# More groups of seven products in the down projection of one hybrid layer

## The chip, the cores and the metric

One core of one Trainium2 chip runs the whole layer as one program. The metric is the device time of one execution in microseconds, lower is better; the kernel before took 1129.32 us (median of 3 runs, 1128.81 to 1129.38).

## The reference, cut to what matters

```python
h2 = rmsnorm(x, norm_ffn)                                  # x: 256 tokens x 2048
x = x + jnp.square(jax.nn.relu(h2 @ w_up)) @ w_down        # w_up 2048 x 8192, w_down 8192 x 2048
return rmsnorm(x, final_norm)
```

Ahead of it stand the projection `w_in`, a chunkwise mLSTM, a forgetting attention, a convolution branch and `w_out`; the change leaves them alone. All is float32.

## The kernel before, in words

**One product.** TensorE multiplies float32r, a float32 rounded to fewer bits. To keep float32 accuracy each operand is split in two: `hi` is the rounded value (written by ScalarE, ACT below) and `lo` what is left (a subtraction on VectorE, DVE below). A product of activations x and weights w is then three matmuls: x_hi by w_hi, x_hi by w_lo, x_lo by w_hi (`mul`, L57). Weights come from HBM in pieces of 128 x 1024 floats (tile `raw`, eight buffers, loaded at L349 by SP's queue), and each piece is split into one `hi` and one `lo`, of which there are five buffers each (NHL = 5): a piece can be split at most five steps ahead of TensorE.

**The feed-forward part.** The 8192 hidden columns are worked in four quarters q of 2048. In each quarter the up projection makes four blocks of 512 hidden columns, and then the down projection multiplies them with 2048 rows of `w_down`. Its 2048 output columns go in two pairs p of 1024 columns; a pair is two blocks of 512 columns, b0 (called x in the order below) and b1 (called y). A pair runs over the four chunks c of 512 hidden values. PSUM has eight banks, four with the tag `mm` and four with `mx`; a block of the down projection holds two (one for each half of the 256 tokens), a block of the up projection four. The two tags change places from one block of the up projection to the next, and from quarter to quarter for the down projection.

**Plain units and groups of seven.** A chunk of a pair is either two plain units (x and y: two steps each, 24 matmuls of 128x512 each) or one group s of seven products after Strassen's scheme (`seven_matmuls`: seven steps of six matmuls, 42 in all). The group needs sums and differences of weight pieces (`sum_task`, L396, four subtractions of 128x1024 on DVE) and of activations (`x_sums`), and seven `hi` and seven `lo` where two plain units need four of each. Three of the seven products (p2, p3, p4) go straight into banks of the pair's own blocks; the four others (p1, p5, p6, p7, called SHARED) collect in four banks of the other tag over all groups of the pair. They are emptied once at the pair's end by `add_up`, one ACT copy per bank (L1361 in the first quarter; L1366, with a DVE addition for each two banks at L1370, in the later ones), and only then can the tag's next block have the banks. The table GROUPS says which chunks are groups; `pair_units` writes the order of units of a pair. In the first three quarters the first pair runs x0 y0 s1 x3 y3 s2, the second y0 x0 s1 x2 y2 x3 y3; in the last quarter the first pair runs x0 y0 s2 x1 y1 x3 y3 and the second has no group.

**What leaves the banks.** `gather` reads a finished block out of PSUM with ACT (L1412, one instruction per bank) and adds it to the residual on DVE (L1418). In the last quarter DVE reads the banks itself (L1485).

**Who sets the order.** A planner inside the kernel keeps a clock for each engine, with costs written in the code, and whenever TensorE's next step is placed it issues for ACT, DVE and POOL those tasks which are ready by its clocks, by priority. The order of TensorE's steps is fixed by `pair_units`. Every engine then runs its instructions strictly in the order issued. `room` tells the planner when PSUM banks and buffers that a step takes are free again. It has no influence on the hardware's waits, which are semaphores.

## Time and profile before

| | |
|---|---|
| median of 3 runs | 1129.32 us |
| the profiled execution, own time | 1129.26 us |
| its span, first to last instruction | 1127.2 us |
[...]
| share of the span: TensorE matmuls, weight loads | 99%, 85% |
| share of the span: DVE, ACT, POOL | 75%, 57%, 2% |
| read from HBM | 211.87 MB, 190 GB/s over the span |

The profiled execution took 0.06 us less than the median of the runs, and 2.06 us of its time lie around the span. TensorE's share counts modelled ends of pipelined matmuls, so it says that matmuls follow each other without a pause, not that each is as fast as it could be. The four down projections lie at 516 to 599, 688 to 771, 860 to 943 and 1032 to 1118 us.

### The profile page before, as it was taken

The page shows a single profiled execution, that of the slowest core. Times are in us where ns is not written, and L with a number is a line of the kernel's source. Part 1 is how long each engine was busy: PE and PEld are TensorE (multiplying, and loading weights), DVE is VectorE, ACT ScalarE, POOL GpSimd, SP SyncE. Part 2 cuts the span into 40 slices and gives each one's busy share as a digit, 9 for nine tenths or more (in the row PEclk, how much of TensorE's full clock was granted, in tenths as well). Part 3 has the DMA queues.
Part 4 walks back from the last instruction along what each step waited for, and adds up shares of the span by engine and source line. Part 5 has one row for each costly group of instructions (what it writes and reads, how often), then busy time and mean ns, then how long its engine had stood idle before and what let it go on. Part 6 is the DMA issues. An engine that isn't in the chain of part 4 may idle for free.

```text
span 1127.2 us, 15562 instructions
## 1 busy us (share of the span) xinstructions
PE 1113.7 (99%) x5836; PEld 954.9 (85%) x5836; DVE 841.0 (75%) x1125; ACT 640.3 (57%) x911; POOL 17.1 (2%) x40
## 2 busy tenths in 40 slices
PE   8999999999999999999999999999999999999996
PEld 7888788888888888888888888888888888888885
DVE  6679998887677785677975677995577997567973
ACT  6444365777775565545664554764454665454552
POOL 1000000010000000000000000000000000000000
PEclk9999999999999999999999999999999999999998
DMA  9766654657555375554776554776554677654742
GB/s 309 253 199 193 187 160 140 181 156 230 182 172 170 126 261 168 168 190 160 233 239 195 179 168 150 232 252 188 187 168 150 219 243 248 187 185 149 245 129 75
DMA packets 130820, 214.98 MB, mean 191 GB/s; under 512 B 6797, under 2 KB 48057, under 8 KB 130361
## 3 DMA queue, kind: packets, MB, share of 16 engines
q1 hardware_dynamic: 130136, 212.93, 58.8%
q8 instruction: 46, 0.75, 0.3%
q10 hardware_dynamic: 608, 1.06, 0.3%
q14 instruction: 30, 0.24, 0.1%
HBM read 211.87 MB, written 2.10 MB: 190 GB/s over the span
## 4 chain that ended last, share of the span: by engine, by line
PE 97%; DMA 1%; issue 1%; DVE 1%; ACT 0%; POOLq 0%; POOL 0%; ACTq 0%; DVEq 0%
PE mm L57 65%; PE mx L57 30%; DMA x<-in_x_dram 1%; DMA rowp<-in_norm_mix_dram 0%; PE mx L984 0%; PE mx L1323 0%; ACT hi L440 0%; PE mx L651 0%; ACT x2t L1525 0%; PE mx L1017 0%; DVE x L637 0%; DVE h L637 0%; DVE x L630 0%; ACT junk L1512 0%; POOLq L1647 0%
## 5 line engine op out<-in xcount | busy, mean ns | idle before, releaser
L461 DVE TENSOR_TENSOR lo<-raw,hi 128x1024 fp32r<-128x1024 f32 x348 | 417.8, 1222 | 218.9 <-issue 136.6
L440 ACT ACTIVATE hi<-raw 128x1024 fp32r<-128x1024 f32 x348 | 364.7, 1058 | 298.4 <-PE mm L57 183.0
L57 PE MATMUL mm<-hi,hid 128*128 128x512 f32 x520 | 163.4, 389 | 0.0
L57 PE MATMUL mm<-x,hi 128*128 128x512 f32 x640 | 156.4, 394 | 0.0
L57 PEld LDWEIGHTS mm<-x,hi 128*128 128x128 f32 x640 | 116.9, 188 | 23.1 <-ACT tmp L559 0.4
L408 ACT ACTIVATE hi<-raw 128x1024 fp32r<-128x1024 f32 x77 | 81.7, 1062 | 73.4 <-PE mm L57 31.4
L57 PE MATMUL mm<-h,hi 128*128 128x512 f32 x512 | 122.7, 391 | 0.2
L57 PE MATMUL mx<-h,hi 128*128 128x512 f32 x512 | 122.1, 390 | 0.0
L57 PEld LDWEIGHTS mm<-hi,hid 128*128 128x128 f32 x520 | 97.6, 188 | 20.2
L57 PEld LDWEIGHTS mm<-h,hi 128*128 128x128 f32 x512 | 94.1, 188 | 19.2 <-DVE x2t L1310 0.9
L57 PEld LDWEIGHTS mx<-h,hi 128*128 128x128 f32 x512 | 94.2, 188 | 18.3
L57 PE MATMUL mx<-hi,hid 128*128 128x512 f32 x328 | 104.3, 389 | 0.0
L412 DVE TENSOR_TENSOR lo<-raw,hi 128x1024 fp32r<-128x1024 f32 x77 | 93.1, 1221 | 14.0 <-ACT hi L408 13.3
L57 PE MATMUL mm<-lo,hid 128*128 128x512 f32 x260 | 101.2, 389 | 0.0
L57 PEld LDWEIGHTS mm<-x,lo 128*128 128x128 f32 x640 | 82.0, 191 | 3.2
L57 PE MATMUL mm<-x,lo 128*128 128x256 f32 x640 | 83.0, 282 | 0.0
L57 PE MATMUL mm<-hi,y 128*128 128x512 f32 x232 | 73.5, 392 | 0.0
L57 PEld LDWEIGHTS mx<-hi,hid 128*128 128x128 f32 x328 | 61.6, 188 | 12.7
L57 PEld LDWEIGHTS mx<-h,lo 128*128 128x128 f32 x512 | 65.6, 191 | 2.5
L57 PEld LDWEIGHTS mm<-h,lo 128*128 128x128 f32 x512 | 65.6, 191 | 2.5
L57 PE MATMUL mm<-h,lo 128*128 128x256 f32 x512 | 66.4, 283 | 0.0
L57 PE MATMUL mx<-h,lo 128*128 128x256 f32 x512 | 66.4, 283 | 0.0
(239 smaller groups left out, 1242.4 us busy)
## 6 DMA issues: line engine op xcount, KB each, us to landing
raw<-in_w_up_dram SPq DMA_DIRECT2D x128, 512.0 KB, 4.2
raw<-in_w_down_dram SPq DMA_DIRECT2D x128, 512.0 KB, 4.9
raw<-in_w_in_dram SPq DMA_DIRECT2D x92, 512.0 KB, 3.6
raw<-in_w_out_dram SPq DMA_DIRECT2D x32, 512.0 KB, 4.2
raw<-in_w_in_dram SPq DMA_DIRECT2D x8, 516.0 KB, 3.6
raw<-in_w_in_dram SPq DMA_DIRECT2D x4, 544.0 KB
x<-in_x_dram SPq DMA_DIRECT2D x8, 256.0 KB, 4.2
x2t<-in_x_dram SPq DMA_DIRECT2D x2, 1024.0 KB
```

The costliest lines, as they stand in the source:

```text
L57: pe.matmul(o, l, r, start=start, stop=stop, skip_group_check=True)
L408: act.activation(hl[i][0], piece(u, h), AF.Copy)
L412: dve.tensor_sub(hl[i][1], piece(u, h), hl[i][0].bitcast(F32))
L440: act.activation(hl[i][0], raws[u, h][0], AF.Copy)
L461: dve.tensor_sub(hl[i][1], raws[u, h][0], hl[i][0].bitcast(F32))
```

## The change

In the first three quarters the second pair gets a second group: its order becomes y0 x0 s1 x3 s2 y3. In the last quarter the first pair gets a second group: x0 y0 x1 s2 y1 s3. The sums of activations for chunk 3 have a buffer of their own (`fourth`, tag `zz`), and those of chunk 2 in the first three quarters are now stored packed, as chunk 1's were. In the last quarter the first two blocks are read from PSUM by `gather`. A bank's last product may now come in any group (`ends`). `room` counts all buffers that a step takes from one rotation, where it looked before at the first one for each.

```diff
--- before.py
+++ after.py
@@ -107,11 +107,13 @@
 
     def room(takes):
 
-        r = 0.0
+        r, more = 0.0, {}
         for b in takes:
             h = b.rot.hist
-            if len(h) >= b.rot.n:
-                for u in h[len(h) - b.rot.n].readers:
+            m = len(h) + more.get(id(h), 0)
+            more[id(h)] = more.get(id(h), 0) + 1
+            if m >= b.rot.n:
+                for u in h[m - b.rot.n].readers:
                     if u.fin is None:
                         return None
                     r = max(r, u.fin + LAT)
@@ -488,7 +490,10 @@
                 xl = stat[:, k, S + j * P:S + (j + 1) * P]
             else:
                 m = {"p5": 0, "p6": 1, "p3": 2, "p7": 3}[p]
-                xh, xl = (g["sums"]()[:, v_, m, ii, :] for v_ in range(2))
+                if m == 3 and g["fourth"]:
+                    xh, xl = (g["fourth"].t[:, v_, ii, :] for v_ in range(2))
+                else:
+                    xh, xl = (g["sums"]()[:, v_, m, ii, :] for v_ in range(2))
             mul(ps, xh, hi[:, ii, :], start and ii == 0, False)
             mul(ps, xh, lo[:, ii, :], False, False)
             mul(ps, xl, hi[:, ii, :], False, stop and ii == 1)
@@ -1182,7 +1187,7 @@
 
         order = [w + str(c) for c in r for w in "xy"]
         for n, c in enumerate(sv):
-            order.insert(3 * n + 2, "s%d" % c)
+            order.insert(2 * n + 3 if 3 in sv else 2 * n + 2 if swap else 3 * n + 2, "s%d" % c)
         if swap:
             order[0:2] = order[1::-1]
         for n, w in enumerate(order):
@@ -1191,7 +1196,8 @@
             rest = "".join(order[n + 1:])
             if w[0] == "s":
                 g = dict(first=c == sv[0], last=c == sv[-1], c=c,
-                         ends=(() if "x" in rest else ("p2", "p4")) + (() if "y" in rest else ("p3",)), **g_of(c))
+                         ends=(() if "x" in rest or "s" in rest else ("p2", "p4")) +
+                              (() if "y" in rest or "s" in rest else ("p3",)), **g_of(c))
                 unit(b1, src, c0 + 512, k, (), seven=(0, g))
                 unit(b0, src, c0, k, (), seven=(1, g))
             else:
@@ -1209,7 +1215,7 @@
     xsum, acc = {}, {}
     oy = seven_of(ob[2], ob[3], "mx", ys, "y")
     pair_units(ob[2], ob[3], w_out, 1024, 0, (YS,), False,
-               lambda c: dict(o=oy, sums=lambda: xsum["y"], packed=False))
+               lambda c: dict(o=oy, sums=lambda: xsum["y"], packed=False, fourth=None))
     U_FFN = len(units)
 
     x2 = {}
@@ -1237,10 +1243,12 @@
 
     z_rot, zz_rot = Rot(2), Rot(2)
 
-    def x_sums(key, c, pk, wb, d, d_lo, prev):
-
+    def x_sums(key, c, pk, wb, d, d_lo, prev, fourth=None):
+
+
+        pr = -0.95 if fourth else -1.85
         zb = Buf(z_rot)
-        m = 3 if pk else 4
+        m = 3 if pk or fourth else 4
 
         def f1():
             zb.t = sbt(pl("late"), [P, 4, S], "z", bufs=2).rearrange("p m (i t) -> p m i t", i=2)
@@ -1252,21 +1260,33 @@
             dve.tensor_sub(t[:, 3], b11, b21)
 
         def f2():
-            t = xsum[key] = sbt(pl("late"), [P, 2, m, 2, P], "xsums%d" % c, F32R)
+            n = 4 if c == 2 else m
+            t = xsum[key] = sbt(pl("late"), [P, 2, n, 2, P], "xsums%d" % (1 if fourth else c), F32R)[:, :, 0:m]
             act.activation(t[:, 0], zb.t[:, 0:m], AF.Copy)
 
         def f3():
             dve.tensor_sub(xsum[key][:, 1], zb.t[:, 0:m], xsum[key][:, 0].bitcast(F32))
 
-        d = t_dve(4 * cd(256), f1, [d] + prev, prio=-1.85, takes=[zb], uses=[wb])
-        a = t_act(ca(256 * m), f2, [d] + prev, prio=-1.85, uses=[zb])
-        r = [t_dve(cd(256 * m), f3, [a], prio=-1.85, uses=[zb])]
+        d = t_dve(4 * cd(256), f1, [d] + prev, prio=pr, takes=[zb], uses=[wb])
+        a = t_act(ca(256 * m), f2, [d] + prev, prio=pr, uses=[zb])
+        r = [t_dve(cd(256 * m), f3, [a], prio=pr, uses=[zb])]
+        if fourth:
+            def at(o):
+                return fourth.t[:, o // S]
+
+            def f4():
+                fourth.t = sbt(pl("late"), [P, 2, 2, P], "zz", F32R, bufs=2)
+                act.activation(at(0), zb.t[:, 3], AF.Copy)
+
+            a = t_act(ca(256), f4, [a], prio=pr, uses=[zb], takes=[fourth])
+            r.append(t_dve(cd(256), lambda: dve.tensor_sub(at(S), zb.t[:, 3], at(0).bitcast(F32)), [a], prio=pr,
+                           uses=[zb]))
         if pk:
             def at(o):
                 return big["hid"][:, 4 * c:4 * c + 2, o + P:o + S]
 
-            a = t_act(ca(256), lambda: act.activation(at(0), zb.t[:, 3], AF.Copy), [a, d_lo], prio=-1.85, uses=[zb])
-            r.append(t_dve(cd(256), lambda: dve.tensor_sub(at(S), zb.t[:, 3], at(0).bitcast(F32)), [a], prio=-1.85,
+            a = t_act(ca(256), lambda: act.activation(at(0), zb.t[:, 3], AF.Copy), [a, d_lo], prio=pr, uses=[zb])
+            r.append(t_dve(cd(256), lambda: dve.tensor_sub(at(S), zb.t[:, 3], at(0).bitcast(F32)), [a], prio=pr,
                            uses=[zb]))
         return r
 
@@ -1339,7 +1359,7 @@
 
 
 
-    GROUPS = {(q, p): ((1, 2), (1,))[p] if q < 3 else ((2,), ())[p] for q in range(4) for p in range(2)}
+    GROUPS = {(q, p): ((1, 2), (1, 2))[p] if q < 3 else ((2, 3), ())[p] for q in range(4) for p in range(2)}
     def packed(q, c):
         return all(c in GROUPS[q, p] for p in range(2))
 
@@ -1415,14 +1435,15 @@
         for j in range(2):
             a.append(t_act(0.62, lambda j=j: f1(j), [b.done[j], rs_t] + a[-1:], prio=-2, takes=[zb] if j == 0 else [],
                            uses=[b.bufs[j]], lag=0.3))
-        t_dve(1.22, lambda: dve.tensor_add(x2[0][:, :, cut(c)], x2[0][:, :, cut(c)], zb.t), a[1:], prio=-0.7,
-              uses=[zb])
+        return t_dve(1.22, lambda: dve.tensor_add(x2[0][:, :, cut(c)], x2[0][:, :, cut(c)], zb.t), a[1:],
+                     prio=-0.7, uses=[zb])
 
     def x2_ap(j, sl):
         return lambda: x2[0][:, j, sl]
 
     fin_t, fsq = [[], []], [[], []]
     ss3, t3 = small(8), small(2)
+    own = Buf(zz_rot)
     for q in range(4):
         t0, t1 = (("mm", "mx"), ("mx", "mm"))[q % 2]
         for c in range(4):
@@ -1452,7 +1473,8 @@
             for i in range(4):
                 chunk["hid%d" % q, 4 * c + i] = d
             if c in GROUPS[q, 0]:
-                chunk["sumshid%d" % q, c] = x_sums(c, c, packed(q, c), wb, done_zz, d, prev)
+                chunk["sumshid%d" % q, c] = x_sums(c, c, packed(q, c), wb, done_zz, d, prev,
+                                                     own if c == 3 else None)
         hid_readers = []
         def down(c, tg):
             return blk("A", 512, lambda: big["hid"], "hid%d" % q, tg)
@@ -1467,7 +1489,7 @@
             b0, b1 = bs[2 * p], bs[2 * p + 1] = down(2 * p, t0), down(2 * p + 1, t0)
             o = seven_of(b0, b1, t1, lambda: big["hid"], "hid%d" % q)
             pair_units(b0, b1, w_down, 1024 * p, KC * q, sv, p == 1,
-                       lambda c: dict(o=o, sums=lambda: xsum[c], packed=packed(q, c)))
+                       lambda c: dict(o=o, sums=lambda: xsum[c], packed=packed(q, c), fourth=own if c == 3 else None))
             got = add_up(p, q, o, q == (3, 2)[p])
             for i, t in enumerate(got):
                 shared[2 * p + i // 2, i % 2] = t
@@ -1479,10 +1501,11 @@
             if q < 3:
                 gather(b, c)
                 continue
+            moved = gather(b, c) if c < 2 else None
             for j in range(2):
                 if c == 3:
                     continue
-                d = t_dve(cd(512), lambda j=j, b=b, c=c: dve.scalar_tensor_tensor(
+                d = moved or t_dve(cd(512), lambda j=j, b=b, c=c: dve.scalar_tensor_tensor(
                     x2[0][:, j, cut(c)], b.bufs[j].t, rs2[:, j:j + 1], x2[0][:, j, cut(c)],
                     op0=OP.mult, op1=OP.add), [b.done[j], rs_t], prio=-2, uses=[b.bufs[j]])
                 if c < 3:
```

The order of ACT's instructions is where the change is seen best. The first piece is ACT's queue in the kernel before, first quarter, at the end of its second pair: `hi` are splits of weights, and the four `fnb` rows empty the four banks of the shared products (p1, p5, p6, p7) for the up projection's next block.

```order
L440 ACTIVATE hi_5532<-raw_5407 128x1024
L440 ACTIVATE hi_5545<-raw_5413 128x1024
L440 ACTIVATE hi_5557<-raw_5433 128x1024
L1361 ACTIVATE fnb_5575<-mx_5486 128x512
L440 ACTIVATE hi_5577<-raw_5495 128x1024
L1361 ACTIVATE fnb_5575<-mx_5508 128x512
L440 ACTIVATE hi_5600<-raw_5506 128x1024
L1361 ACTIVATE fnb_5575<-mx_5536 128x512
L440 ACTIVATE hi_5621<-raw_5530 128x1024
L1361 ACTIVATE fnb_5575<-mx_5521 128x512
L440 ACTIVATE hi_5640<-raw_5543 128x1024
```

The four copies stand one by one between splits of weights for the plain units x2, y2, x3 and y3, which TensorE still has to run after the group.

The same place in the change: `mx_5514`, `mx_5540` and `mx_5527` are the banks of p5, p6 and p7, `mm_5442` is a bank of the pair's first block, `mm_5395` and `mm_5396` are those of its second block, whose last unit is y3. The `hi` rows are already weights of the next up projection; `hi_5729` takes the buffer that the last step of y3 frees, being the fifth split after that step's own.

```order
L1432 ACTIVATE z_5641<-mm_5442,st_99 128x512
L442 ACTIVATE hi_5700<-raw_5620 128x1024
L442 ACTIVATE hi_5718<-raw_5630 128x1024
L1381 ACTIVATE fnb_5638<-mx_5514 128x512
L442 ACTIVATE hi_5729<-raw_5649 128x1024
L1432 ACTIVATE z_5734<-mm_5395,st_99 128x512
L1381 ACTIVATE fnb_5638<-mx_5540 128x512
L1432 ACTIVATE z_5734<-mm_5396,st_99 128x512
L1381 ACTIVATE fnb_5638<-mx_5527 128x512
L442 ACTIVATE hi_5780<-raw_5673 128x1024
L442 ACTIVATE hi_5792<-raw_5679 128x1024
```

The copies of p6 and p7 now stand behind `hi_5729` and between the two reads of block y.

The last quarter in the change, ACT's queue at the end of its first pair, which two plain blocks follow: `hi_9787` is the split for the group's last product (p4), `mx_9470` its bank, the four next `hi` belong to plain units of the next block, and `mm_9613`, `mm_9635`, `mm_9662` are shared banks; the next block takes the banks of `mm_9613` and `mm_9635` for its two halves.

```order
L410 ACTIVATE hi_9787<-raw_9633 128x1024
L442 ACTIVATE hi_9789<-raw_9656 128x1024
L442 ACTIVATE hi_9799<-raw_9671 128x1024
L442 ACTIVATE hi_9805<-raw_9683 128x1024
L442 ACTIVATE hi_9811<-raw_9701 128x1024
L1432 ACTIVATE z_9769<-mx_9470,st_99 128x512
L442 ACTIVATE hi_9818<-raw_9754 128x1024
L1386 ACTIVATE zz_9763<-mm_9635 128x512
L1386 ACTIVATE zz_9846<-mm_9662 128x512
```

The copy that frees the second bank stands behind six splits and a read, where before the change four plain units lay between the group and that block.

## Rows read from the trace of the kernel before

**Rows 1.** The page: busy time, share of the span and instructions of each engine.

```profile
PE 1113.7 (99%) x5836; PEld 954.9 (85%) x5836; DVE 841.0 (75%) x1125; ACT 640.3 (57%) x911; POOL 17.1 (2%) x40
```

**Rows 2.** Chain that ended last, first down projection: start us, us, engine, tile, line, count.

```profile
535.47 13.60 PE mm L57 x60
549.07 1.36 PE mx L57 x6
...
576.27 23.12 PE mm L57 x102
599.39 0.68 PE mx L57 x3
```

**Rows 3.** Waits of the weight loads: us in total, times, longest us.

```profile
PEld mm L57 <- DVE x2t L1310: 0.9, 2, 0.5
...
PEld mm L57 <- DVE lo L461: 0.2, 1, 0.2
```

**Rows 4.** Windows, first, second and last down projection: busy us (count) by engine, clock, DMA.

```profile
516.40:599.40 83.00, 83.00 (x367) 68.71 (x367) 69.56 (x63) 51.47 (x60) 0.00 (x0) 1.00 0.62 204
...
688.40:771.40 83.00, 83.00 (x368) 68.71 (x367) 73.96 (x67) 51.62 (x60) 0.00 (x0) 1.00 0.62 203
...
1032.40:1118.20 85.80, 85.78 (x379) 70.68 (x377) 63.73 (x74) 42.79 (x58) 0.93 (x1) 1.00 0.42 136
```

**Rows 5.** Groups by line and form: the work that groups of seven add, whole span.

```profile
L408 ACT ACTIVATE hi<-raw 128x1024 fp32r<-128x1024 f32 x77 | 81.7, 1062 | 73.4 <-PE mm L57 31.4 <-DVE raw L396 23.6 <-PE mx L57 14.6
L412 DVE TENSOR_TENSOR lo<-raw,hi 128x1024 fp32r<-128x1024 f32 x77 | 93.1, 1221 | 14.0 <-ACT hi L408 13.3
L396 DVE TENSOR_TENSOR raw<-raw 128x1024 f32<-128x1024 f32 x44 | 53.7, 1221 | 0.5
```

**Rows 6.** Timeline, DVE: start us, us, line, operation; p4's `lo` is the second.

```profile
534.77 4.62 DVE L461 TENSOR_TENSOR lo<-raw,hi 128x1024 fp32r<-128x1024 f32 x4
...
553.44 1.22 DVE L412 TENSOR_TENSOR lo<-raw,hi 128x1024 fp32r<-128x1024 f32 x1
```

**Rows 7.** Timeline, ACT: splits, reads of a block, copies of shared banks.

```profile
533.50 3.89 ACT L440 ACTIVATE hi<-raw 128x1024 fp32r<-128x1024 f32 x4
...
550.12 1.25 ACT L1412 ACTIVATE z<-mm,st 128x512 f32<-128x512 f32 x2
...
577.27 0.58 ACT L1361 ACTIVATE fnb<-mx 128x512 f32<-128x512 f32 x1
577.75 1.05 ACT L440 ACTIVATE hi<-raw 128x1024 fp32r<-128x1024 f32 x1
...
584.07 0.58 ACT L1361 ACTIVATE fnb<-mx 128x512 f32<-128x512 f32 x1
```

**Rows 8.** Timeline at p4's end and y0's start: TensorE's steps and ACT's read.

```profile
555.93 0.39 PE L57 MATMUL mm<-lo,hid 128*128 128x512 f32 x1
...
556.84 0.61 PE L57 MATMUL mm<-hi,hid 128*128 128x512 f32 x2
557.26 0.69 ACT L1412 ACTIVATE z<-mm,st 128x512 f32<-128x512 f32 x1 [0.30 <-PE mm L57]
```

**Rows 9.** Timeline, first block of the first up projection: it waits for banks.

```profile
425.32 0.41 PEld L57 LDWEIGHTS mm<-h,hi 128*128 128x128 f32 x2
425.52 1.27 DVE L1310 TENSOR_TENSOR x2t<-x2t,mm 128x512 f32<-128x512 f32 x2
425.54 4.55 PE L57 MATMUL mm<-h,hi 128*128 128x512 f32 x16
...
426.85 2.82 PEld L57 LDWEIGHTS mm<-h,hi 128*128 128x128 f32 x13 [0.41 <-DVE x2t L1310]
```

**Rows 10.** Line L349, the weight loads: who waited for them, us and times.

```profile
  ACT hi L440: 0.5, 1
  ACT hi L408: 0.2, 1
```

**Rows 11.** TensorE's timeline: its longest pause at full clock, its last matmul.

```profile
14.11 0.44 PE L651 MATMUL mx<-ident,x 128*128 128x128 f32 x2 [1.58 <-DVE x L630]
...
1117.80 0.39 PE L57 MATMUL mm<-hi,hid 128*128 128x512 f32 x1
```

**Rows 12.** Windows around both: the column behind POOL is the granted clock.

```profile
10.00:15.00 5.00, 3.42 (x29) 3.09 (x27) 4.35 (x12) 4.17 (x9) 1.50 (x5) 1.00 1.05 400
1118.50:1120.50 2.00, 0.00 (x0) 0.00 (x0) 1.27 (x4) 1.02 (x4) 0.33 (x1) 1.00 0.80 272
1121.00:1127.00 6.00, 0.00 (x0) 0.00 (x0) 0.88 (x2) 1.44 (x2) 0.11 (x1) 0.50 0.50 175
```

## Prediction

> **What bounds the kernel now.** I read the page's busy shares first [rows 1]: TensorE's matmuls fill 99% of the span, DVE 75%, ACT 57%. Then the chain that ended last, in order of time, through a down projection [rows 2]. The reader should see that it is TensorE alone, without a pause: 60 matmuls of 512 columns in 13.60 us, 6 in 1.36, 102 in 23.12, always 0.2267 us each. Third, the waits of the weight loads [rows 3]: in the whole feed-forward part TensorE waits for another engine in one place, 0.9 us for two banks at the start of the first up projection. So a matmul left out there is worth 0.2267 us as long as nothing else becomes late, and the question is what does. Fourth, the windows of the down projections [rows 4]: DVE is busy 69.6 of 83 us in the first and 74.0 in the second, ACT 51.5 in both. These are the stretches into which the change puts more work for both.
>
> **The change, part by part.**
>
> *Matmuls removed.* A chunk as a group takes 42 matmuls in place of 48. Four chunks change (one in each quarter), so 4 x 6 x 0.2267 = **5.44 us less**, all on the path.
>
> *Splits and subtractions added.* Each such group adds three splits to ACT (1.06 each), and three `lo` and four subtractions of weight pieces to DVE (1.22 each) [rows 5]. Back to back they cost less: four `lo` in 4.62 us are one each (4.62 - 1.22) / 3 = 1.133, and four splits in 3.89 us are 0.944 [rows 6, 7]. From y0 to p4 of s2 the second pair gives TensorE 150 matmuls, 34.0 us. DVE starts it five steps ahead, so it has 15 `lo`, 8 subtractions and two to four additions of results to do, 25 to 27 x 1.133 = 28.3 to 30.6 us. It fits on the whole, but not at every step. Before the change p4's `lo`, in the first pair's s2, ends at 554.66 and TensorE uses it at 555.93 [rows 6, 8], 1.27 us later. In the second and third quarter one or two additions of shared banks, 1.133 us each, come ahead of it in the new order; in the first there are none (the copies go straight to their place), and in the last the group before p4 has plain units between. Each of the two places thus costs between 0 and 2 x 1.133 - 1.27 = 1.0 us; I take 0.4, nearer to one addition than to two: **0.8 us more**.
>
> *The shared banks.* This is the term that decides. Before, four plain units (21.8 us) lie between the last group and the block that needs its shared banks; the last copy is issued at 584.07, the block starts at 599.39 [rows 2, 7], so 15 us are to spare. Now only y3 lies between, 24 matmuls or 5.44 us, and ACT's order puts the copies of p6 and p7 behind `hi_5729`, which waits for a buffer that the last step of y3 frees. Let E be the time when TensorE is through with y3. ACT follows 0.20 us later (the next step starts at 557.06, ACT's read at 557.26 [rows 8]); then come the split (0.944), a read of block y (two in 1.25, so 0.575 [rows 7]) and the copy of p6 (0.58 to its end): E + 2.30. A weight load that waited for a bank starts some 0.05 us after the read that frees it, and its matmul 0.22 after the load starts (425.32 against 425.54, 426.85 against the end of the reads at 426.79 [rows 9]). So the third bank's matmul runs at E + 2.57, where it would have run at E + 0.45: 2.12 us. Then ACT reads y's other bank and copies p7: the copy of p6 holds ACT for 0.48 (577.27 to 577.75 [rows 7]), the read 0.575, and the copy ends 0.58 later, at E + 3.35. The fourth matmul runs at E + 3.62 in place of E + 2.80, another 0.82. The first quarter loses **2.94 us**. In the second and third quarter one copy alone stands behind that split, and its bank is the fourth: E + 2.57 in place of E + 0.68, **1.89 us each**. In the last quarter, with H the start of p4's split: five splits back to back end ACT's hold at H + 4.72, a read at 5.30, a split at 6.24, the copy at 6.82, and the second bank's matmul runs at H + 7.09. TensorE has p4's `lo` at the soonest at H + 1.06 + 1.22 + 0.27 = H + 2.55 for its second matmul, so is through with p4 and three matmuls of the next block at H + 4.36: 2.73 us if p4 comes at the soonest, less if it comes later. Between this and the 1.89 I take **2.4**. Together 9.1 us. The nearest measured thing of the kind bears the price: at 425.54 sixteen matmuls took 4.55 us, where 15 x 0.227 + 0.39 = 3.79 would do [rows 9], so such a wait does reach TensorE in full. The bounds of the term: nothing, if ACT is through before E as it is now, and 12 us if each of the four places is as bad as the first.
>
> [...]
>
> *What costs nothing.* In the last quarter `x_sums` for chunk 3 adds six DVE instructions and two on ACT, and `gather` moves two blocks' reads to ACT. None is longer than 1.22 us, so DVE gains less than 7.4 us of work, beside 22 us in which it is idle there [rows 4], and chunk 3's group comes last in its pair; without that cover it would be those 7.4. Packing chunk 2's sums exchanges one long instruction for two shorter. The loads: a group frees its four `raw` buffers later than two plain units do, and SP's queue, which is strictly in order, holds the loads behind them; in the whole kernel splits waited 0.7 us for loads [rows 10], so I take nothing, with 1 us as the bound for each added group. The end of the kernel, after the last matmul, keeps its instructions.
>
> **The sum.** 1129.26 (the profiled execution; 0.06 below the median of the runs) - 5.44 + 0.8 + 9.1 = **1133.7 us**.
>
> **The rivals.**
>
> *The copies are hidden after all* (faster). If ACT's split ahead of them does not wait for y3's last step, or ACT reaches the copies of p6 and p7 before E, nothing is left of the 9.1 us. For it: the copies are short (0.58), TensorE leaves p6's bank 6.8 us ahead of E (p4 and y3), and ACT idles much [rows 4]. Against it: the order is strict and the split stands ahead of them in three quarters. It decides where ACT's copy of p7 ends before E + 0.4. Time: 1129.26 - 5.44 + 0.8 = 1124.6.
>
> *Only part of it.* If in each place ACT gets by without one split's time (0.944, for example because a buffer comes free a step earlier), 3.8 us fall away, and with them the sum is 1129.9, no difference that can be told. A measurement of this kernel tells about 0.2%, 2.3 us, from no change.
>
> *DVE becomes the bound* (slower still). A group asks 11 x 1.133 = 12.5 us of DVE in 9.52 us of TensorE. If the lead of five steps is spent before each added group, each loses up to 2.95 us, in place of the 0.8 in the sum: 1133.7 - 0.8 + 11.8 = 1144.7 at worst, about 1139 with half. For it: DVE's 74 busy us in the second quarter [rows 4] grow by 8.5. Against it: the plain unit x3 between the groups, and the balance above.
>
> *TensorE's clock falls in the new pauses.* The trace shows full clock held over a pause of 1.58 us, and lost between 1120.5 and 1121, some 2.3 to 2.8 us after the last matmul ended at 1118.19 [rows 11, 12]. The pauses I expect are 1.7 to 2.2 us without a matmul, between the two. [...]
>
> *The change does not do what it says*: if the planner's order made the added groups run as plain units, the time would stay. The order of instructions shows them, so it gets no chance of its own.
>
> **How the numbers follow.** The forecast, within some 2 us, 0.70; part of it, 0.11; the copies hidden, 0.05; DVE as the bound, 0.07; the clock, 0.07. Faster by over 0.2% is the hidden copies alone, 0.05; within 0.2% the partial case, 0.11; slower the rest, 0.84. The range, 1130.3 to 1138.5, leaves out the hidden copies, most of the DVE case and about half of the others' far ends; it takes in DVE at 1.0 in both its places and the last quarter at 2.7 or 1.9.
>
> **What the profile after would show.** Right: weight loads of `mx<-h,hi` or `mm<-h,hi` waiting for ACT's copies of shared banks, about 2.1 and 0.8 us at the first up projection after a down projection, 1.9 at the next two; in the last down projection 2.4 us ahead of the second block's bank; elsewhere 0.2267 us per matmul, and 24 matmuls fewer. Weight loads waiting for `lo` for under 1 us in the second and third quarter. Wrong: no PSUM wait there, a clock under 0.99 before the last matmul, or waits for `lo` in sum above those for copies.

## The result and the profile after

The changed kernel takes 1136.37 us (median of 6 runs, 1133.84 to 1137.2), the kernel before beside it 1129.23 (6 runs, 1128.81 to 1129.42): a ratio of 1.0059, with a 95% interval of 1.0048 to 1.0069. The profiled execution took 1134.14 us, 1131.7 of them its span. The times of the change spread over 3.4 us, those of before over 0.6, and that will matter below.

TensorE's matmuls are 24 fewer, and DVE and ACT have more to do, as was reckoned (against [rows 1]):

```profile
PE 1111.2 (98%) x5812; PEld 950.7 (84%) x5812; DVE 874.0 (77%) x1160; ACT 655.6 (58%) x932; POOL 17.0 (2%) x40
```

Where the time went is read from TensorE's timeline by stages: from the first matmul of a down projection to the first of the next up projection, and so on to the last matmul. This table is worked out from those starts, in the profiled execution of each kernel (the four on the right are experiments, told below):

| stage, us | before | after | again | copies_early | plain_last | early_and_costs |
|---|---|---|---|---|---|---|
| first down projection | 82.98 | 81.63 | 81.63 | 81.62 | 84.08 | 81.63 |
| second up projection | 89.04 | 91.97 | 93.25 | 89.04 | 89.04 | 89.04 |
| second down projection | 82.99 | 82.06 | 82.06 | 82.27 | 85.07 | 81.63 |
| third up projection | 89.04 | 90.88 | 90.90 | 89.03 | 89.04 | 89.04 |
| third down projection | 82.99 | 82.06 | 82.07 | 82.26 | 85.11 | 81.62 |
| fourth up projection | 89.04 | 90.90 | 90.90 | 89.04 | 89.04 | 89.04 |
| last down projection | 85.48 | 86.66 | 88.26 | 84.97 | 88.23 | 84.12 |

Six matmuls less are 6 x 0.2267 = 1.36 us less in each down projection. The first gives 1.35 back in full; the second and third give 0.93, so 0.43 is lost in each; the last is 1.18 longer instead, so 2.54 is lost. And the up projections, in which the change moves no matmul, are longer by 2.93, 1.84 and 1.86 us. These differences sum to 4.60 us. The own time grew by 1134.14 - 1129.26 = 4.88; the rest, 0.3, lies around these stages.

The waits of the weight loads name the places. In before, TensorE waited for no engine there ([rows 3]). Now (us in total, times, longest us):

```profile
PEld mm L57 <- ACT zz L1386: 4.6, 2, 2.7
PEld mx L57 <- ACT fnb L1381: 3.1, 2, 2.2
...
PEld mx L57 <- ACT zz L1386: 2.0, 1, 2.0
...
PEld mm L57 <- DVE lo L414: 0.6, 1, 0.6
PEld mx L57 <- DVE lo L414: 0.6, 1, 0.6
```

L1381 and L1386 are `add_up`'s copies of shared banks, the first in the first quarter (`fnb`), the second in the later ones (`zz`): 9.7 us of waits in five places, of which the first quarter has two. L414 is the `lo` of a group. This is TensorE's timeline at the end of the first down projection (start us, us, engine, line, operation, tiles, count, and in brackets the idle time before):

```profile
597.65 0.39 PE L57 MATMUL mm<-hi,hid 128*128 128x512 f32 x1
597.88 0.61 PE L57 MATMUL mx<-h,hi 128*128 128x512 f32 x2
600.25 0.50 PE L57 MATMUL mx<-h,hi 128*128 128x512 f32 x1 [1.76 <-ACT fnb L1381]
601.31 1.90 PE L57 MATMUL mx<-h,hi 128*128 128x512 f32 x7 [0.56 <-ACT fnb L1381]
```

The up projection begins at 597.88, right behind y3, and does two matmuls in the banks of p1 and p5. The third waits for p6's bank until 600.25, the fourth for p7's until 601.31. ACT's timeline shows what it did meanwhile:

```profile
596.32 0.57 ACT L1381 ACTIVATE fnb<-mx 128x512 f32<-128x512 f32 x1
598.07 1.06 ACT L442 ACTIVATE hi<-raw 128x1024 fp32r<-128x1024 f32 x1 [1.18 <-PE mm L57]
599.04 0.67 ACT L1432 ACTIVATE z<-mm,st 128x512 f32<-128x512 f32 x1
599.61 0.59 ACT L1381 ACTIVATE fnb<-mx 128x512 f32<-128x512 f32 x1
600.09 0.69 ACT L1432 ACTIVATE z<-mm,st 128x512 f32<-128x512 f32 x1
600.65 0.61 ACT L1381 ACTIVATE fnb<-mx 128x512 f32<-128x512 f32 x1
```

The reader should look at the 1.18 us of idle time ahead of 598.07. ACT had nothing to do, and p6's bank had long been complete (its last matmul started at 590.85), but the next instruction in its queue was a split that waited for TensorE's last step (`<-PE mm L57`). Only behind it come the reads of block y and the copies of p6 (599.61) and p7 (600.65). So the third matmul starts 0.05 us after p6's copy ends (600.20), and the fourth 0.05 after p7's (601.26).

In the last quarter the same copies stand behind five splits and a read of a block, in ACT's timeline:

```profile
1073.71 3.89 ACT L442 ACTIVATE hi<-raw 128x1024 fp32r<-128x1024 f32 x4
1077.50 0.67 ACT L1432 ACTIVATE z<-mx,st 128x512 f32<-128x512 f32 x1
1078.07 1.04 ACT L442 ACTIVATE hi<-raw 128x1024 fp32r<-128x1024 f32 x1
1079.02 1.07 ACT L1386 ACTIVATE zz<-mm 128x512 f32<-128x512 f32 x2
```

TensorE's timeline has the pause that this makes, 2.62 us from the start of one matmul to the start of the next:

```profile
1077.03 0.39 PE L57 MATMUL mm<-hi,hid 128*128 128x512 f32 x1
1079.65 0.50 PE L57 MATMUL mm<-hi,hid 128*128 128x512 f32 x1 [2.23 <-ACT zz L1386]
```

The other loss, 0.43 us in the second and third quarter, is p4's `lo`. DVE's timeline in the second quarter, and behind the dots ACT's split for p4:

```profile
757.96 3.49 DVE L414 TENSOR_TENSOR lo<-raw,hi 128x1024 fp32r<-128x1024 f32 x3
761.36 1.22 DVE L398 TENSOR_TENSOR raw<-raw 128x1024 f32<-128x1024 f32 x1
762.79 1.23 DVE L1390 TENSOR_TENSOR fnb<-fnb,zz 128x1024 f32<-128x1024 f32 x1 [0.20 <-ACT zz L1386]
763.93 1.22 DVE L414 TENSOR_TENSOR lo<-raw,hi 128x1024 fp32r<-128x1024 f32 x1
...
762.67 1.06 ACT L410 ACTIVATE hi<-raw 128x1024 fp32r<-128x1024 f32 x1
```

And TensorE's there:

```profile
764.67 0.39 PE L57 MATMUL mx<-hi,hid 128*128 128x512 f32 x1
765.20 0.50 PE L57 MATMUL mx<-lo,hid 128*128 128x512 f32 x1
765.54 0.39 PE L57 MATMUL mx<-hi,hid 128*128 128x512 f32 x1
```

The `lo` (763.93) ends at 765.15, and the matmul that reads it starts at 765.20, where 764.90 was its turn: 0.30 us. The next one follows after 0.34 us in place of 0.2267, another 0.11, so that 0.41 of the 0.43 stand in these rows. Two things make the `lo` late. One is the addition of shared banks (L1390), which comes ahead of it after 0.20 us in which DVE waited for ACT's copy. The other is the last of the group's four subtractions (L398), which makes p4's piece and stands behind three `lo` of other products. It ends at 762.58; the split for p4 can only then start (762.67) and ends at 763.73, so without the addition the `lo` would have started at about 763.77, an estimate from the 0.03 us by which a `lo` that waited for its split follows it (760.95 to 760.98 in `copies_early`, below). The addition thus has 0.16 of the 0.30 us, the late subtraction the other 0.14.

Last, the window of the second down projection: DVE is busy 78.99 of 82 us, where it was 73.96 of 83 [rows 4].

```profile
689.90:771.90 82.00, 81.86 (x361) 67.44 (x361) 78.99 (x73) 54.09 (x62) 0.00 (x0) 1.00 0.58 191
```

### The profile page after: what moved, and what is told of

It reads as the page before. It is cut to its first block, busy times and chain, and to the rows that moved or that the text cites. A ratio compares the mean times of both kernels' runs of the same rounds, so it can differ in the third digit from the quotient of the medians.

```text
span 1131.7 us, 15579 instructions
## 1 busy us (share of the span) xinstructions
PE 1111.2 (98%) x5812; PEld 950.7 (84%) x5812; DVE 874.0 (77%) x1160; ACT 655.6 (58%) x932; POOL 17.0 (2%) x40
## 3 DMA queue, kind: packets, MB, share of 16 engines
q10 hardware_dynamic: 608, 1.06, 0.3%
## 4 chain that ended last, share of the span: by engine, by line
PE 94%; DMA 2%; ACT 1%; issue 1%; DVE 1%; POOLq 0%; POOL 0%; ACTq 0%; DVEq 0%
PE mm L57 64%; PE mx L57 30%; DMA raw<-in_w_in_dram 1%; DMA x<-in_x_dram 1%; ACT hi L442 0%; DMA rowp<-in_norm_mix_dram 0%; ACT z L1432 0%; ACT zz L1386 0%; PE mx L1343 0%; PE mx L989 0%; DMA rowp<-in_norm_ffn_dram 0%; DVE lo L414 0%; DVE lo L463 0%; ACT x2t L1548 0%; PE mx L1022 0%
## 5 line engine op out<-in xcount | busy, mean ns | idle before, releaser
L463 DVE TENSOR_TENSOR lo<-raw,hi 128x1024 fp32r<-128x1024 f32 x332 | 397.7, 1223 | 192.6 <-issue 129.3
L442 ACT ACTIVATE hi<-raw 128x1024 fp32r<-128x1024 f32 x332 | 346.5, 1057 | 263.9 <-PE mm L57 166.7
L410 ACT ACTIVATE hi<-raw 128x1024 fp32r<-128x1024 f32 x105 | 111.5, 1062 | 93.2 <-PE mm L57 34.9
L57 PE MATMUL mm<-hi,hid 128*128 128x512 f32 x488 | 155.3, 389 | 2.2 <-ACT zz L1386 2.2
L57 PE MATMUL mm<-x,hi 128*128 128x512 f32 x640 | 156.4, 394 | 0.0
L414 DVE TENSOR_TENSOR lo<-raw,hi 128x1024 fp32r<-128x1024 f32 x105 | 126.5, 1223 | 13.1 <-ACT hi L410 12.5
L57 PEld LDWEIGHTS mm<-x,hi 128*128 128x128 f32 x640 | 116.9, 188 | 23.1 <-ACT tmp L564 0.4
L57 PE MATMUL mx<-h,hi 128*128 128x512 f32 x512 | 123.0, 391 | 3.9 <-ACT fnb L1381 2.3
L57 PE MATMUL mm<-h,hi 128*128 128x512 f32 x512 | 123.2, 391 | 1.7 <-ACT zz L1386 1.5
L57 PEld LDWEIGHTS mx<-h,hi 128*128 128x128 f32 x512 | 94.1, 188 | 23.3 <-ACT fnb L1381 3.1
L57 PEld LDWEIGHTS mm<-h,hi 128*128 128x128 f32 x512 | 94.0, 188 | 21.0 <-ACT zz L1386 2.0
L57 PEld LDWEIGHTS mm<-hi,hid 128*128 128x128 f32 x488 | 91.6, 188 | 21.6 <-ACT zz L1386 2.7
L57 PE MATMUL mx<-hi,hid 128*128 128x512 f32 x304 | 98.5, 389 | 0.0
L57 PE MATMUL mm<-lo,hid 128*128 128x512 f32 x244 | 95.1, 390 | 0.1
L57 PEld LDWEIGHTS mm<-x,lo 128*128 128x128 f32 x640 | 82.0, 191 | 3.2
L57 PE MATMUL mm<-x,lo 128*128 128x256 f32 x640 | 83.0, 282 | 0.0
L398 DVE TENSOR_TENSOR raw<-raw 128x1024 f32<-128x1024 f32 x60 | 73.3, 1222 | 0.7
L57 PE MATMUL mm<-hi,y 128*128 128x512 f32 x232 | 73.5, 392 | 0.0
L57 PEld LDWEIGHTS mm<-h,lo 128*128 128x128 f32 x512 | 65.6, 191 | 2.5
L57 PEld LDWEIGHTS mx<-h,lo 128*128 128x128 f32 x512 | 65.7, 191 | 2.5
L57 PEld LDWEIGHTS mx<-hi,hid 128*128 128x128 f32 x304 | 57.1, 188 | 11.8
L57 PE MATMUL mm<-h,lo 128*128 128x256 f32 x512 | 66.4, 283 | 0.0
```

The costliest lines, as they stand in the source:

```text
L57: pe.matmul(o, l, r, start=start, stop=stop, skip_group_check=True)
L398: sums[i] = t_dve(C_LO, lambda: dve.tensor_sub(piece(*o), piece(*l), piece(*r)), after + [arrival(*l), arrival(*r)], prio=-1)
L410: act.activation(hl[i][0], piece(u, h), AF.Copy)
L414: dve.tensor_sub(hl[i][1], piece(u, h), hl[i][0].bitcast(F32))
L442: act.activation(hl[i][0], raws[u, h][0], AF.Copy)
L463: dve.tensor_sub(hl[i][1], raws[u, h][0], hl[i][0].bitcast(F32))
```

## The experiments

The theory is the prediction's: the added groups give TensorE 5.44 us, and ACT's late copies of the shared banks take more than that away, because of where they stand in ACT's queue. One rival is DVE: a group asks more of it than TensorE's time for the group allows, and the waits for copies only cover that. Another is TensorE's clock, since the median stands 2.2 us above the profiled execution, which no wait of that trace explains. All edits are to the changed kernel.

**The change once more** (no edit). Expected:

> The changed kernel once more, unaltered, for its spread: its six runs lay between 1133.84 and 1137.2 us with a mean granted clock between 0.997 and 0.995, the kernel before between 1128.81 and 1129.42. Waits for banks alone (theory A): the profile shows the same pauses each time and all runs stay within 1 us of 1134. Clock (theory C): in some runs TensorE's clock falls after a pause; runs lie at 1134 where the mean clock is 0.997 and 1 to 3 us above where it is 0.996 or 0.995, and a profile of such a run shows a stretch at 0.5 right behind one of the five pauses of 0.8 to 2.6 us. DVE (theory B): the spread comes from DVE, and waits for lo differ between profiles.

Measured: 1135.48 us (5 runs, 1135.2 to 1136.77), before on the same chip 1128.95 (16 runs), ratio 1.006 [1.0047, 1.0073]. The profiled execution was one of the longer ones, 1136.77 us, and its waits for copies are those of the first profile: 4.6, 3.1 and 2.0 us. What differs is the column behind POOL in the windows, the granted clock. The first block is this run, around the first quarter's pauses and, behind the dots, after the last quarter's; the second is the first profile of the change at the same two places:

```profile
596.00:600.40 4.40, 2.64 (x11) 1.69 (x9) 3.59 (x3) 3.23 (x7) 0.00 (x0) 1.00 0.99 339
600.50:603.80 3.30, 2.78 (x7) 2.23 (x8) 1.22 (x1) 0.71 (x2) 0.00 (x0) 0.50 0.99 372
...
1081.80:1085.10 3.30, 3.30 (x10) 2.53 (x9) 2.23 (x2) 1.07 (x2) 0.00 (x0) 0.50 0.99 357
```

```profile
598.00:601.40 3.40, 1.08 (x5) 0.34 (x3) 2.63 (x3) 3.19 (x5) 0.00 (x0) 1.00 1.05 401
601.40:604.80 3.40, 3.40 (x17) 2.83 (x18) 0.63 (x1) 1.23 (x2) 0.00 (x0) 1.00 0.81 302
...
1080.40:1083.80 3.40, 3.40 (x16) 2.77 (x16) 3.28 (x4) 1.55 (x2) 0.00 (x0) 1.00 1.01 340
```

The clock fell behind the long pause of the first quarter (597.81 to 599.96; it is at 0.50 from 600.5 on) and behind that of the last (1078.05 to 1080.67; at 0.50 from 1081.8 on), so each time after TensorE had resumed, by 0.5 and 1.1 us at the most. TensorE's timeline has the price of a matmul there:

```profile
1082.08 1.05 PE L57 MATMUL mm<-hi,hid 128*128 128x512 f32 x2
1082.94 0.63 PE L57 MATMUL mm<-lo,hid 128*128 128x512 f32 x1
1083.36 1.05 PE L57 MATMUL mm<-hi,hid 128*128 128x512 f32 x2
```

Three matmuls take 1083.36 - 1082.08 = 1.28 us, 0.427 each in place of 0.2267. By the table of stages the two falls cost 93.25 - 91.97 = 1.28 us and 88.26 - 86.66 = 1.60. So the first profile has the price of the waits alone, and this one that of the falls besides. The pauses are the same in both to 0.01 us (from start to start 2.15 and then 1.07 us in the first quarter, 2.62 in the last): the same pause lost the clock in one execution and kept it in the other.

**ACT's copies early.**

```diff
-            ts.append(t_act(0.6, f1 if q else f, [o["done"][x]] + ts[-1:], prio=-0.8,
-                            takes=[wb] if q and m % 2 == 0 else [], uses=[o["extra"][x]], lag=1.5))
+            ts.append(t_act(0.6, f1 if q else f, [o["done"][x]] + ts[-1:], prio=-1.5,
+                            takes=[wb] if q and m % 2 == 0 else [], uses=[o["extra"][x]], lag=0.8))
```

The copies go ahead of splits in the planner's choice, and are offered sooner. The computation and every instruction stay; ACT's order moves, and what follows from it in the planner's order for DVE. Expected:

> The planner gives the copies of the shared banks the priority -1.5 in place of -0.8 and lets them be issued 0.8 us after their product instead of 1.5; nothing else. Theory A (banks wait for late copies): the waits for the copies, 9.7 us in the profile of the change, vanish; what is left of the 5.44 us saved is reduced by some 2 us of waits for lo, so 1125.5 us, about 4 below the kernel before. Theory B (DVE is the bound): no copy is in the way, time stays at 1133 or above, waits for lo grow by as much as waits for copies fall. Theory C (clock): without pauses of over 1 us all runs lie within 0.5 us of each other and the mean clock is that of the kernel before.

Measured: 1125.55 us (6 runs, 1124.92 to 1125.67), ratio to before 0.9969 [0.9958, 0.9981]. No wait for a copy is left; the up projections are back at 89.04 us each, and the spread is 0.75 us. ACT's copies in the first quarter now stand among the splits, from 585.62 on; this is the last of the four:

```profile
593.96 0.59 ACT L1381 ACTIVATE fnb<-mx 128x512 f32<-128x512 f32 x1
```

It ends at 594.55, 3.1 us before the up projection starts (597.66). So the four places' loss was the order of ACT's queue, not ACT's amount of work. What is left over are waits for `lo`, now in three quarters and longer each: 82.27, 82.26 and 84.97 in the table, where 81.63, 81.63 and 84.12 would be all of the gain, so 2.1 us. DVE's timeline in the second quarter shows why; behind the dots are ACT's split for p4 and the matmul that waited:

```profile
755.17 3.49 DVE L414 TENSOR_TENSOR lo<-raw,hi 128x1024 fp32r<-128x1024 f32 x3
758.58 1.22 DVE L398 TENSOR_TENSOR raw<-raw 128x1024 f32<-128x1024 f32 x1
759.71 1.22 DVE L1390 TENSOR_TENSOR fnb<-fnb,zz 128x1024 f32<-128x1024 f32 x1
760.98 1.23 DVE L414 TENSOR_TENSOR lo<-raw,hi 128x1024 fp32r<-128x1024 f32 x1
...
759.89 1.06 ACT L410 ACTIVATE hi<-raw 128x1024 fp32r<-128x1024 f32 x1 [0.28 <-DVE raw L398]
...
762.26 0.50 PE L57 MATMUL mx<-lo,hid 128*128 128x512 f32 x1 [0.34 <-DVE lo L414]
```

The last subtraction (L398) again stands behind three `lo` and ends at 759.79; the split waits for it and ends at 760.95, and the `lo` starts 0.03 us later, so the addition at 759.71 isn't what holds it. The third quarter has the same order; in the last quarter two additions stand ahead of the `lo`.

**One part alone: the last quarter's second group.**

```diff
-    GROUPS = {(q, p): ((1, 2), (1, 2))[p] if q < 3 else ((2, 3), ())[p] for q in range(4) for p in range(2)}
+    GROUPS = {(q, p): ((1, 2), (1,))[p] if q < 3 else ((2, 3), ())[p] for q in range(4) for p in range(2)}
```

> Of the change only the last quarter's second group; the first three quarters keep three groups. Theory A: one group saves 1.36 us and one pause of 2.6 us between matmuls costs 2.4, so 1130.3 us. Theory C: if the clock falls in this pause, the longest of the five, part of the runs lie 1 to 2 us higher, to 1132.5; if the falls belong to the pauses ahead of the up projections, all runs lie within 0.5 us. Theory B: below 1129, since DVE has the least work in the last quarter.

Measured: 1131.51 us (11 runs, 1129.88 to 1131.87), ratio 1.0019 [1.0011, 1.0028]. The profiled execution took 1130.28, at full clock through the pause; its last down projection is 86.65 us, as in the change (86.66), and all other stages are those of before. The eleven times lie in two clumps, four from 1129.88 to 1130.43 and seven from 1131.07 to 1131.87. Their middles, 1130.29 and 1131.68, lie 1.4 us apart, near the 1.60 that the fall at this place cost in `again`; that the upper clump are executions with a fall was inferred from times and mean clocks (0.997 to 0.998 against 0.996), not seen in a trace.

**The other part alone: the first three quarters.**

```diff
-    GROUPS = {(q, p): ((1, 2), (1, 2))[p] if q < 3 else ((2, 3), ())[p] for q in range(4) for p in range(2)}
+    GROUPS = {(q, p): ((1, 2), (1, 2))[p] if q < 3 else ((2,), ())[p] for q in range(4) for p in range(2)}
```

> Of the change only the fourth groups of the first three quarters; the last quarter keeps its one group. Theory A: saves 3 x 1.36 = 4.08 us; pauses cost 2.9, 1.9 and 1.9, waits for lo 0.9, so 1132.8 us. Theory C: if the falls of the clock belong to these pauses, part of the runs lie 1 to 2 us higher, to 1135; else all lie within 0.5 us. Theory B: waits for lo exceed those for copies.

Measured: 1133.61 us (5 runs, 1132.0 to 1134.02), ratio 1.0038 [1.0024, 1.0051]. The waits for copies are those of the change's first three quarters (3.1 us in two, 2.0 and 2.0), and the profiled execution has the clock at 0.50 from 600.5 on, by which its second up projection took 93.29 us in place of 91.97. The two parts add up: with the fall taken off (93.29 - 91.97 = 1.32, by which this one stage agrees with the change by construction) the stages of this one sum to 3.43 us over before, those of the last quarter alone to 1.17, and those of the change to 4.60.

**The pauses filled.** At the four places the first matmul of the waiting block is repeated 8, 6, 6 and 9 times, each time starting the bank anew, so that the same product is written over itself and what is computed doesn't change; 29 matmuls more, and no copy earlier. The lines for the up projections, to which those of the last quarter are alike:

```diff
+                if s0 and d["src"] is w_up and d["c0"] in FILL_UP and d["b"].kind == "B":
+                    for _ in range(FILL_UP[d["c0"]]):
+                        mul(b.bufs[0].t, hi[:, ii, 0:P], stat[:, k, :], True, False)
```

> The changed kernel with TensorE kept at work in its long pauses: the first matmul of the block that will wait is repeated 8 times at the first up projection behind a down projection, 6 times at the next two, 9 times in the last quarter. Each repeat overwrites the same bank with the same product, so the result stays; the 29 repeats take 6.6 us of TensorE, nearly all within pauses that are there anyway. Nothing else moves. Theory C (the spread of the change's runs is the clock, which falls after pauses): no run shows a mean clock under 0.997, all runs lie within 0.6 us of 1134.0, below the median of the bare change by 1.5 us although there is more work. Theory A without C: the same spread as the change, 1134 to 1137, and no gain. Against both: if repeats delay the matmuls behind them, 1 us or more above the fastest runs of the change.

Measured: 1134.0 us (5 runs, 1133.85 to 1134.32), before 1129.15 (15 runs on that chip), ratio 1.0043 [1.003, 1.0055]. More matmuls, and the median is 1.5 to 2.4 us below those of the change, at the time which the change has when the clock stays; and the spread is 0.5 us in place of 3.4. The page counts the 29, and the rest of the pauses remains as waits:

```profile
PE 1117.3 (99%) x5841; PEld 956.0 (84%) x5841; DVE 873.8 (77%) x1160; ACT 655.4 (58%) x932; POOL 17.1 (2%) x40
```

```profile
PEld mx L57 <- ACT fnb L1389: 1.2, 2, 0.9
PEld mm L57 <- ACT zz L1394: 1.2, 2, 0.6
```

So the part of the loss above the profiled execution is the clock, and it is gone with the pauses filled although no copy comes earlier: the five executions have mean clocks of 0.997 and 0.998, those of the change 0.995 to 0.997.

**More plain work behind the last group.** In the second pair of the first three quarters the two groups go directly behind y0 and x0, and both plain units of chunk 3 come last: y0 x0 s1 s2 x3 y3.

```diff
-            order.insert(2 * n + 3 if 3 in sv else 2 * n + 2 if swap else 3 * n + 2, "s%d" % c)
+            order.insert(2 * n + 3 if 3 in sv else n + 2 if swap else 3 * n + 2, "s%d" % c)
```

> In the first three quarters the second pair runs its two groups back to back and its plain units last: y0 x0 s1 s2 x3 y3. Theory A (only the 5.44 us of TensorE's work behind the last group decide): with 10.9 us there the copies are done in time, the 6.7 us of waits ahead of the three up projections vanish, and the time is that of the change's fast runs less 6.7, 1127.3 us. Theory B (two groups in a row overdraw DVE: 22 x 1.133 = 24.9 us in 19.0 us of TensorE, with a lead of five steps): waits for lo of 1.5 to 3 us for each of the three quarters take their place, 1132 to 1136 us. The last quarter's pause of 2.4 us and its possible fall of the clock stay in both.

Measured: 1135.85 us (5 runs, 1135.73 to 1137.58), ratio 1.0064 [1.0052, 1.0077]. The theory of late copies alone would have had a gain here, and it is right on its own ground: the three up projections are back at 89.04 us. But the down projections take 84.08, 85.07 and 85.11 us in place of 81.63, and the waits change their engine:

```profile
PEld mm L57 <- DVE lo L414: 4.0, 3, 1.8
PEld mx L57 <- DVE lo L414: 3.7, 3, 1.8
...
PEld mm L57 <- ACT hi L410: 1.7, 2, 0.8
```

The splits (L410) for which TensorE waits are themselves behind DVE's subtractions: in the first quarter the split at 585.64 starts 0.09 us after a subtraction ends. Without a plain unit between the groups DVE's 11 instructions per group (11 x 1.133 = 12.5 us) don't fit into TensorE's time (42 x 0.2267 = 9.52), and 2.45, 3.44 and 3.48 us per quarter go to that. The rival of DVE is thus a true one of the same size, and it is x3 between the two groups, as the change has it, that keeps it away. (The profiled execution, 1137.58, also had a fall in the last quarter: its mean clock is 0.98 from 1030 to 1125, where the change's first profile has 1.00 from 1035.7 to 1122.5.)

**The planner's costs as measured.** The planner takes 1.06 us for a split and 1.22 for a `lo` or a subtraction, the length of a row. Back to back they cost 0.944 and 1.133 [rows 6, 7].

```diff
-    C_HI, C_LO = 1.06, 1.22
+    C_HI, C_LO = 0.95, 1.135
```

> The planner's costs as measured (0.95 and 1.135 us), but the copies of shared banks keep their priority and lag. Theory A: the copies still stand behind splits that wait for TensorE, so pauses of nearly 2 us stay ahead of each up projection and in the last quarter; waits for lo vanish. 1131.5 us where the clock holds, up to 3 us more where it falls. If the planner's wrong costs were what made the copies late, the pauses vanish too and the time is 1123.6.

Measured: 1131.26 us (11 runs, 1130.67 to 1131.53), ratio 1.0018 [1.0009, 1.0027]. All waits of a group's `lo` are gone (the first three down projections take 81.63 us each), the first quarter's two waits became one, and one remains at each of the three up projections, which take 90.89, 90.87 and 90.91 us. In the last down projection two waits remain (0.7 and 1.5 us) and cost 1.94 us. All eleven executions lie within 0.9 us, less than the 1.28 and 1.60 that a fall cost in `again`, so by their times these single pauses of 1.92 us from start to start lost the clock in none of them; the one trace shows none.

```profile
PEld mm L57 <- ACT zz L1386: 4.1, 3, 2.0
...
PEld mx L57 <- ACT fnb L1381: 2.0, 1, 2.0
PEld mx L57 <- ACT zz L1386: 2.0, 1, 2.0
```

**Both: copies early, and costs as measured.**

> Copies early as in the run of that name, and besides the planner is told what the trace shows two instructions in a row to cost: 0.95 us for a split on ACT and 1.135 for one on DVE, in place of 1.06 and 1.22. Only the order of instructions changes. Theory B (what is left after the copies are out of the way, 1.7 us, is waits for lo that come from order, not from DVE's capacity): these waits vanish, the whole 5.44 us are saved, 1123.6 us. If DVE's capacity is the limit, the waits stay and so does the time of the run with early copies, 1125.5.

Measured: 1123.43 us (5 runs, 1123.21 to 1123.73), ratio to before 0.9949 [0.9937, 0.9962]. This beats the kernel before by 5.7 us, and the change by 13. Every down projection of the table is that of before less 1.35 to 1.37, and every up projection is that of before: all 5.44 us of the removed matmuls arrive, and no wait of TensorE for a copy or a `lo` of a group is left. DVE's timeline has the last subtraction (757.56) behind one `lo` in place of three, and p4's `lo` (the second of the two at 758.70) ahead of the addition of shared banks, where the change has it behind:

```profile
756.43 1.22 DVE L414 TENSOR_TENSOR lo<-raw,hi 128x1024 fp32r<-128x1024 f32 x1
757.56 1.22 DVE L398 TENSOR_TENSOR raw<-raw 128x1024 f32<-128x1024 f32 x1
758.70 2.50 DVE L414 TENSOR_TENSOR lo<-raw,hi 128x1024 fp32r<-128x1024 f32 x2
...
762.64 1.22 DVE L1390 TENSOR_TENSOR fnb<-fnb,zz 128x1024 f32<-128x1024 f32 x1
```

The subtraction ends (758.78) 3.18 us ahead of the matmul that needs the `lo` (761.96); in the change it was 764.90 - 762.58 = 2.32, and in `copies_early` 761.76 - 759.79 = 1.97, where split and `lo` behind it take 2.47 us (759.79 to 762.26).

## Why the prediction was right, and where it missed

**Matmuls removed: right.** 1.35 or 1.36 us in each down projection wherever nothing else is late (the first in the change, all four in the last experiment).

**The shared banks: right, in mechanism and size.** It gave 2.94, 1.89, 1.89 and 2.4 us, 9.1 in all. The stages show 2.93, 1.84, 1.86 and 2.54, which is 9.17. The order of events was the one written out: TensorE's last step, the split that waits for it (598.07), a read, the copy of p6, a read, the copy of p7. Only its last link was drawn wrongly: a matmul that waited starts 0.05 us behind the copy that frees its bank, where 0.27 was reckoned, but the matmuls after it follow later: the next one after 0.34 us in place of 0.2267 (1079.99 behind 1079.65, as 765.54 behind 765.20), and by the stages, less the wait of the matmul itself, 0.14 to 0.18 us a place. The two errors, 0.22 us and these, nearly cancel, and that they do is luck; so is the exact size in the last quarter, where 2.4 was a choice between 1.89 and 2.73. That the rest of the price could be worked out from rows of a kernel that has no such wait comes from ACT's queue keeping its order, as the rows from 596.32 to 600.65 have it: once the order of its instructions is known, their durations do the rest.

**p4's `lo`: right in size, by luck.** 0.4 us in each of two quarters, against 0.43 twice. The 0.4 was a choice between 0 and 1.0, from 1.27 us to spare and one or two additions ahead. There is one addition, and by that balance one addition, with the 0.20 of waiting for the copy, would cost 1.133 + 0.20 - 1.27 = 0.06. But the 1.27 didn't carry over: in the change's first quarter, where no addition comes ahead, the `lo` ends 0.7 us before its turn (590.61 against 591.30), and in the second the late subtraction alone puts it 0.14 behind. The step that the prediction left out is the chain from the last subtraction through its split to the `lo`; `copies_early` loses 1.3 of its 2.1 us to it.

**What costs nothing: right.** The last quarter alone loses 1.18 + 1.36 = 2.54 us, its one wait for a bank; `x_sums` for chunk 3, the reads moved to ACT and the loads don't show as waits of TensorE.

**The sum.** 1133.7 against 1134.14 in the profiled execution without a fall. The stages give +4.60, the sum +4.46; the 0.3 around the stages had no term.

**The clock: the step that fell short.** The prediction made it a rival of 7%, for all the new pauses. In truth it is neither none nor all. What a fall costs no row of the kernel before shows, since no matmul stands there at the lower clock; so the range's upper end had no measured price of a fall in it. In `again` a fall cost 1.28 and 1.60 us, with the clock at 0.50 for 3.3 us at least and 0.427 us for a matmul in place of 0.2267. Falls were seen behind the first quarter's pair of pauses and behind the last quarter's, the longest, and in no trace behind the single ones of 1.92 us. And it varies from execution to execution. Of the eleven timed executions of the change, two lie at 1133.84 and 1134.14, five from 1135.2 to 1135.72, four from 1136.77 to 1137.2. With some 1.3 to 1.6 us per fall these would be none, one and two; the mean clocks go with that (0.997, 0.996, 0.995), and traces were taken of one of the first kind and one of the last, so that the kind in the middle is inferred. The median of the first six, 1136.37, lies between an execution of the second kind and one of the third; it is 2.7 us above the forecast, outside the "within some 2 us" to which 0.70 was given, and `again`, with a median of 1135.48, is 1.8 above it. What was told as one case out of five is a part of most executions. The statement that a mean clock under 0.99 would be its sign was too coarse: the profiled execution of `again`, with two falls in 1134 us, has 0.995. And in `filled` 29 useless matmuls in the pauses won 1.5 to 2.4 us.

**The other rivals.** Copies hidden after all did not happen in the change, but it is what the two numbers in `copies_early` make of it: that rival's 1124.6, with 0.8 for `lo` in it, stands beside 1125.55 measured, with 2.1 for `lo`. DVE as the bound did not happen either, for the reason given against it, the plain unit x3; `plain_last` takes that away and pays 2.5 to 3.5 us per quarter, where up to 2.95 per group had been worked out.

What stays open: more exact costs in the planner move the last subtraction ahead of two `lo`, and with that the waits go; which of its choices moved first was not followed. And why the clock fell in some executions and held in others at the same pauses is not shown by any run.

## What to carry to other kernels

A unit that needs fewer matmuls also leaves less time behind it, and what has to be emptied at its end must find its place in another engine's queue: look at what stands ahead of it there and what that waits for, since an engine can sit idle at a split, as ACT did here for 1.18 us, while the copy that everyone needs is next in line. Before giving up such a change, move that copy, and give the planner the distance at which instructions follow each other (0.944 and 1.133 us here), not the length of one (1.06 and 1.22). Where an operand comes late, follow it back through everything that makes it, not only to the instruction just ahead of it. And where TensorE gets a new pause, compare distributions: here pauses of 2.15 and 2.62 us from start to start had a fall of the clock behind them in one profile, which cost 1.28 and 1.60 us, and none in another, so that a single profile can be the one without it.

## What was not expected of the hardware

The same pause, 2.62 us from start to start with nothing on TensorE in between, kept the clock at 1.00 in one execution and was followed by 3.3 us at 0.50 in another, with matmuls at 0.427 us in place of 0.2267. Of two kernels whose copies are equally late, the one with 29 more matmuls had the lower median, 1134.0 us against 1136.37 and 1135.48. And behind a wait the matmul started within 0.05 us of the end of what it waited for, and the next one 0.34 us behind it in place of 0.2267.
